# A two-layer decoder trunk on one Trainium2 core: low parts of weights made by accumulating loads, and a third pair of rows in sevens

## The chip, the cores and the metric

The program runs on one core of a Trainium2 chip. That core has a matrix engine (PE, with its weight-load half PEld), a vector engine (DVE), an activation engine (ACT), a general engine (POOL), and a queue engine (SP) that issues loads and stores. The metric is the device time in microseconds of one execution. Three executions of the kernel before took 2597.22, 2598.99 and 2599.99 us, so the median is 2598.99 us.

## The reference, cut to what matters

The reference is a trunk of two layers over 256 tokens of width 2048, all in float32. Layer 0 has a retention mixer, layer 1 a short gated convolution, and each is followed by a SwiGLU block of inner width 5632:

```
def swiglu(h, w_in, w_out):
    a, b = jnp.split(h @ w_in, 2, axis=-1)
    return (jax.nn.silu(a) * b) @ w_out
...
        x = (x + g1 * y).astype(x.dtype)
        h = (rms_norm(x, norm2_g[i]) * (1.0 + sc2) + sh2).astype(x.dtype)
        x = (x + g2 * swiglu(h, ffn_w_in[i], ffn_w_out[i])).astype(x.dtype)
    return rms_norm(x, final_g).astype(x.dtype)
```

The change is in the SwiGLU block of the last layer alone (the "last stage" below). Its input product multiplies 256 x 2048 tokens by 2048 x 11264 weights, its output product 256 x 5632 by 5632 x 2048.

## The kernel before, in words

**Three products for one.** Float32 factors are split into a high part, rounded to the type `float32r` that PE multiplies in one pass, and a low part, which is the factor minus its high part. Every product is then three: high by high, high by low and low by high (`thrice`). Activations are split once. Weights are split as they come: SP loads them from one long array, `w_all`, in blocks of 128 x 2048 (1 MB each, tile `raw`, three buffers, line L372), and `prepare` makes them ready in **pieces** of 128 x 1024. For a piece ACT copies `raw` into the tile `hi` (L402, this rounds), and DVE subtracts `hi` from `raw` into the tile `lo` (L405). `hi` and `lo` have four buffers each (`PART_BUFS`), and in the last stage a piece is prepared three pieces before PE takes it (`ahead_now`, `AHEAD + 1`). So ACT may begin piece n + 3 when PE has read the last of piece n - 1 and begins n.

**How the last stage is cut.** The weights are taken in **groups**. An input group gathers 1024 columns (512 of each half of the input weights) over all 2048 rows of weights. It goes through eight **row pairs** (two times 128 rows by 2 x 512 columns, which is one block of 1 MB). Part 0 has four input groups and two output groups, part 1 six input groups and two output groups. An output group has ten row pairs in part 0, twelve in part 1, where the very last group ends with three row pairs taken column by column, the tail.

**Common pairs and sevens.** A common row pair is two pieces, each with 12 matmuls of 128x512. A row pair in **sevens** (class `Seven`) is a product of two by two blocks (two halves of the tokens, two row blocks, two column blocks), done with seven block products where the plain way takes eight. That is 21 matmuls against 24. The seven block products need sums and differences of weight blocks, which DVE makes in `prepare`: a 128x1024 difference (L391) and two of 128x512 (L395, L397). Its pieces are four (numbers 2, 3, 4, 5), three of 1024 columns and one of 512, with 6, 6, 6 and 3 matmuls. They also need sums of the activations: for input pairs `made_in_sums` makes them once ahead of the first input group, for output pairs `turned` makes them as the pair's activations come out. Which pairs are in sevens is in the line

```
IN_SEVEN, OUT_SEVEN, TURNS_AT, BESIDE_CB, BESIDE_SUMS = (3, 5), (2, 4, 6), 2, 40, 48
```

**Between groups.** After the last seven of a group its four side banks are mixed (`mixed_sums`: one ACT copy, four DVE additions), after the last row pair DVE adds the four main banks (L1315), ACT takes silu twice (L1319), DVE multiplies twice (L1320). Two row pairs into the next group (`TURNS_AT`) PE turns the result with eight transposes (L1329), and ACT and DVE split it (L1333, L1334).

**What sets the order.** PE's instructions stand in the order of the program text. The instructions of ACT, DVE, POOL and SP are put into an order per engine by the framework's scheduler when the program is built. Each engine then works through its list strictly in that order, so an instruction that waits holds up all that stand behind it.

Of the kernel before, what the change touches and what calls it, by code (L numbers as in the profile page):

```python
# [10 lines left out]
F32 = mybir.dt.float32  # L11
# [3 lines left out]
ALU = mybir.AluOpType  # L15
# [162 lines left out]
def last_out(part):  # L178

    first, n = part * LAST_TILES[0], LAST_TILES[part]  # L180
    order = list(range(n // 2))
    if not part:
        a, b = order[-2:]
        order = order[:5] + [a, order[6], b, order[5], order[7]]
    rows = [(i, [first + 2 * i, first + 2 * i + 1]) for i in order]
    out = []
    for c in range(0, D, 2 * DV):
        cols, rest = [c, c + DV], 0
        if part and c + 2 * DV == D:
            rest = TAIL_ROWS // 2  # L190
        out.append(in_pairs(cols, rows[: len(rows) - rest], OUT_SEVEN))
# [65 lines left out]
def trunk(ctx: ExitStack, tc: tile.TileContext, x_in, c_in, pos_in, w_mod, cols_in, gain_in, tab_in, w_all, out):  # L257
# [12 lines left out]
    def tmp(tag, shape=(P, S), dtype=F32, pool=work, bufs=None):  # L270
        return pool.tile(list(shape), dtype, tag=tag, name=name(tag), bufs=bufs)
# [104 lines left out]
    def prepare(between=None):  # L376
        if prepared[0] == len(pieces):
            return
        _, piece = pieces[prepared[0]]
        prepared[0] += 1  # L380
        if piece in (0, 2):
            if not fetched:
                fetch()
            raws[:] = [fetched.pop(0)]
            while first <= units[0] < early and len(fetched) < RAW_BUFS - 1 and n_fetched[0] < w_all.shape[0]:
                fetch()
        whole = raws[0]
        b = [whole[:, i : i + DV] for i in range(0, CHUNK, DV)]
        raw = whole[:, :HALF] if piece in (0, 4) else whole[:, HALF:]
        if piece == 2:  # L390
            nc.vector.tensor_tensor(differences, whole[:, DV : 3 * DV], whole[:, : 2 * DV], op=ALU.subtract)  # L391
        elif piece == 3:
            raw = differences
        elif piece == 4:
            nc.vector.tensor_tensor(b[1], b[2], differences[:, :DV], op=ALU.subtract)  # L395
        elif piece == 5:
            nc.vector.tensor_tensor(b[3], b[3], b[1], op=ALU.subtract)  # L397
# [4 lines left out]
        nc.scalar.copy(hi, raw)  # L402
        if between:
            between()
        nc.vector.tensor_tensor(lo, raw, hi.bitcast(F32), op=ALU.subtract)  # L405
        ready.append((hi, lo, width))

    prepared, ahead_now = [0], [AHEAD]
# [714 lines left out]
    def turn(t, c):  # L1123
# [8 lines left out]
    needed(1, GT2)  # L1132
    in_cb = const.tile([P, D], F32R, tag="cb", name="in_cb")
    tokens_sums = [
        v.rearrange("p (i n) -> p i n", i=2) for v in (in_cb[:, : 6 * P], in_cb[:, 6 * P : 12 * P])
    ] + [mpool.tile([P, 2, 3 * P], F32R, tag="sums_of_tokens", name="sums_of_tokens")]

    def tokens_sums_of(a11, a21, a12, a22, third, others):

# [17 lines left out]
    def made_in_sums():  # L1157

        tmp("beside_sums", (P, BESIDE_SUMS), bufs=1)
        for i in IN_SEVEN:  # L1160
            both = tmp("u512", (P, 2, S), pool=mpool, bufs=3)
            for n in range(2):
                k = 2 * i + n
                high, low = [h[k].bitcast(F32)[:, v, :] for v in range(2)]
                nc.vector.tensor_tensor(both[:, n, :], high, low, op=ALU.add)
            tag = "low" if in_sums else "u"
            in_sums[i] = [tmp(tag, (P, 2, P), F32R, bufs=3) for _ in range(3)]
            tokens_sums_of(*parts(both), h[2 * i][:, :, P:], in_sums[i])

    def three(v):  # L1170
        return [v[:, :, n * P : (n + 1) * P] for n in range(3)]

    turns = [lambda t=t, c=c: turn(t, c) for c in range(4) for t in range(2)]

# [136 lines left out]
    def last_input(groups, pairs, seven):  # L1311

        ours, extra = gathered(groups, h, 0, in_sums)
        for (t, j), pt in ours.items():
            nc.vector.tensor_tensor(extra[t, j], pt, extra[t, j], op=ALU.add)  # L1315
        ms = []
        for t in range(2):
            m = extra[t, 0]
            nc.scalar.activation(m, m, AF.Silu)  # L1319
            nc.vector.tensor_tensor(m, m, extra[t, 1], op=ALU.mult)  # L1320
            ms.append(m)

        def turned():
            for n, (dst, of) in enumerate(zip(pairs, seven)):
                pt = bank()
                for i in range(2):
                    for t, m in enumerate(ms):
                        c = slice((2 * n + i) * P, (2 * n + i + 1) * P)
                        nc.tensor.transpose(pt[:, i, t * P : (t + 1) * P], m[:, c], ident)  # L1329
                if of is not None:  # L1330
                    both = tmp("u512", (P, 2, S), pool=mpool, bufs=3)
                    nc.scalar.copy(both, pt)
                nc.scalar.copy(dst[:, :, 0, :], pt)  # L1333
                nc.vector.tensor_tensor(dst[:, :, 1, :], pt, dst[:, :, 0, :].bitcast(F32), op=ALU.subtract)  # L1334
                if of is not None:
                    tokens_sums_of(*parts(both), dst[:, 0, :, P:], [of])

        waiting.append(turned)

    def last_output(part, c, groups, act, base):  # L1340
# [14 lines left out]
            for (t, j), v in extra.items():  # L1355
                gated(t, c + j, v, 0)

        sums = {i: three(v) for i, v in zip(OUT_SEVEN, tokens_sums)}
# [27 lines left out]
    for part in range(2):  # L1386
        n = LAST_TILES[part] // 2
        mid = mids(LAST_TILES[part]) if part else first_mid
        if not part:
            first_rows(mid[-2:])  # L1390
            made_in_sums()
            ahead_now[0] = AHEAD + 1
        for i, groups in enumerate(LAST_IN[part]):
            seven = [tokens_sums[OUT_SEVEN.index(q)] if q in OUT_SEVEN else None for q in (2 * i, 2 * i + 1)]
# [41 lines left out]
```

## Time and profile before

| what | value |
|---|---|
| median of three runs | 2598.99 us |
| profiled execution, its own time | 2600.71 us |
| profiled execution, span of the trace | 2598.8 us |
| last stage, first difference of weights (L391) to the span's end | from 1927.9 us on |
| granted PE clock in the profiled run | 0.999 |
| PE busy share of the span | 99% |
| DVE, ACT, POOL busy shares | 83%, 50%, 5% |

The profile is of one execution. Its span lies 1.9 us below that execution's own time and 0.2 us below the median of the three runs. Times in the trace are counted from the span's start. A matmul's duration in the rows overlaps with the next matmul's, since matmuls are pipelined, so PE's pace is read from the distance between starts and not from durations. The same is true, to a lesser degree, of DVE and ACT. A row of the waits says which instruction waited for which, then the sum in us, the number of times and the longest.

### The profile page before, as it was taken

To read this page: it belongs to the slowest core of one execution; us is meant where nothing else is said; L and a number is where in the kernel's file an instruction comes from. 1 tells how busy PE (TensorE), PEld (TensorE's weight loads), DVE (VectorE), ACT (ScalarE), POOL (GpSimd) and SP (SyncE) were. 2 spreads that over 40 slices of the span, in tenths; PEclk is the share of its full clock that TensorE was granted. 3 is DMA by queue.
4 is the path that set the end of the run, shared out by engine and by line. 5 is a ranking of instruction groups with operands and counts; after the bars stand their busy time and mean duration, and the time that the engine had idled before them with its cause. 6 is when DMAs were issued, how large, how long until landed. Compare 5 with 4: busy or idle time off the path is not lost.

```text
span 2598.8 us, 36365 instructions
## 1 busy us (share of the span) xinstructions
PE 2567.0 (99%) x14211; PEld 2241.0 (86%) x14211; DVE 2157.4 (83%) x2702; ACT 1289.4 (50%) x1768; POOL 125.7 (5%) x232
## 2 busy tenths in 40 slices
PE   7999999999999999999999999999999999999998
PEld 6898889888889888888888898888998888888886
DVE  7988978887698887777777889988988888888877
ACT  5544543444456454334444454444565554555554
POOL 0000000110000000100001001000000000000000
PEclk9999999999999999999999999999999999999999
DMA  9975668877676888787778868877845565554653
GB/s 399 387 290 221 255 246 300 299 261 276 244 284 247 330 325 305 298 299 302 294 284 296 299 237 313 326 290 277 305 171 204 190 217 203 184 207 182 221 200 146
DMA packets 96686, 689.55 MB, mean 265 GB/s; under 512 B 10737, under 2 KB 12161, under 8 KB 13441
## 3 DMA queue, kind: packets, MB, share of 16 engines
q1 hardware_dynamic: 96514, 687.23, 71.1%
q8 instruction: 111, 1.82, 0.3%
q14 instruction: 61, 0.50, 0.1%
HBM read 685.08 MB, written 2.11 MB: 264 GB/s over the span
## 4 chain that ended last, share of the span: by engine, by line
PE 84%; DVE 7%; DMA 5%; issue 2%; ACT 1%; ACTq 0%; POOLq 0%; POOL 0%; DVEq 0%; SPq 0%
PE bank L447 25%; PE bank L450 14%; PE bank L461 12%; PE bank L460 12%; PE bank L462 12%; DMA raw<-w_all 4%; DVE lo L405 3%; DMA raw<-w_mod 2%; PE bank L496 2%; PE bank L495 1%; PE bank L494 1%; PE bank L627 1%; PE bank L629 1%; PE bank L628 1%; DVE raw L755 1%
## 5 line engine op out<-in xcount | busy, mean ns | idle before, releaser
L402 ACT CAST hi<-raw 128x1024 fp32r<-128x1024 f32 (+1 forms) x944 | 973.1, 1039 | 1037.0 <-PE bank L462 385.6
L405 DVE TENSOR_TENSOR lo<-raw,hi 128x1024 fp32r<-128x1024 f32 (+1 forms) x944 | 1129.9, 1203 | 347.4 <-ACT hi L402 340.0
L447 PE MATMUL bank<-h,hi 128*128 128x512 f32 x2016 | 699.2, 390 | 0.0
L450 PE MATMUL bank<-h,lo 128*128 128x256 f32 x2016 | 568.4, 282 | 0.0
L447 PEld LDWEIGHTS bank<-h,hi 128*128 128x128 f32 x2016 | 378.3, 188 | 79.2
L460 PE MATMUL bank<-hi,h 128*128 128x512 f32 x1072 | 420.1, 392 | 1.8 <-DVE rm L739 1.8
L461 PE MATMUL bank<-lo,h 128*128 128x512 f32 x1072 | 418.3, 390 | 0.7 <-DVE lo L405 0.7
L462 PE MATMUL bank<-hi,h 128*128 128x512 f32 x1072 | 417.6, 390 | 0.0
L318 DVE SCALAR_TENSOR_TENSOR raw<-raw,cb 128x2048 f32<-128x2048 f32 x160 | 365.6, 2285 | 23.2 <-DMA raw<-w_mod 22.9
L450 PEld LDWEIGHTS bank<-h,lo 128*128 128x128 f32 x2016 | 381.0, 189 | 0.0
L447 PE MATMUL bank<-mid,hi 128*128 128x512 f32 x922 | 319.8, 390 | 0.0
L450 PE MATMUL bank<-mid,lo 128*128 128x256 f32 x922 | 260.1, 282 | 0.4 <-DVE lo L405 0.4
L462 PEld LDWEIGHTS bank<-hi,h 128*128 128x128 f32 x1072 | 201.4, 188 | 42.6
L460 PEld LDWEIGHTS bank<-hi,h 128*128 128x128 f32 x1072 | 201.8, 188 | 41.8 <-DVE rm L739 2.4
L461 PEld LDWEIGHTS bank<-lo,h 128*128 128x128 f32 x1072 | 201.9, 188 | 39.9 <-DVE lo L405 1.1
L447 PEld LDWEIGHTS bank<-mid,hi 128*128 128x128 f32 x922 | 173.0, 188 | 36.2
L450 PEld LDWEIGHTS bank<-mid,lo 128*128 128x128 f32 x922 | 174.3, 189 | 0.7 <-DVE lo L405 0.7
L447 PE MATMUL bank<-rm,hi 128*128 128x512 f32 x496 | 172.6, 390 | 0.0
L496 PE MATMUL bank<-h,lo 128*128 128x256 f32 x512 | 146.2, 286 | 5.2 <-DVE lo L405 5.2
L494 PE MATMUL bank<-h,hi 128*128 128x256 f32 x512 | 145.6, 284 | 3.2 <-ACT h L783 3.2
L495 PE MATMUL bank<-h,hi 128*128 128x256 f32 x512 | 145.6, 284 | 0.7 <-DVE h L784 0.7
L450 PE MATMUL bank<-rm,lo 128*128 128x256 f32 x496 | 139.9, 282 | 0.0
(248 smaller groups left out, 3092.4 us busy)
## 6 DMA issues: line engine op xcount, KB each, us to landing
raw<-w_all SPq DMA_DIRECT2D x456, 1024.0 KB, 4.9
raw<-w_mod SPq DMA_DIRECT2D x192, 1024.0 KB, 5.3
x<-x_in SPq DMA_DIRECT2D x4, 512.0 KB, 5.5
out<-xt SPq DMA_DIRECT2D x4, 512.0 KB, 3.0
decay<-tab_in SPq DMA_DIRECT2D x8, 128.0 KB, 2.7
x<-gate_row SPq DMA_DIRECT2D x2, 512.0 KB, 4.4
last_gain<-gain_in SPq DMA_DIRECT2D x1, 1024.0 KB, 4.6
cols<-cols_in SPq DMA_DIRECT2D x1, 152.0 KB, 8.5
```

The source lines that it names most:

```text
L318: nc.vector.scalar_tensor_tensor(raw, raw, 1.0, cb, op0=ALU.mult, op1=ALU.mult, accum_out=total)
L402: nc.scalar.copy(hi, raw)
L405: nc.vector.tensor_tensor(lo, raw, hi.bitcast(F32), op=ALU.subtract)
L447: nc.tensor.matmul(pt, hi, h, start=fresh and k == g.ks[0], stop=False, skip_group_check=True)
L450: nc.tensor.matmul(pt[:, 1, :], lo, h[:, 0, :], start=False, stop=last and k == g.ks[-1], skip_group_check=True)
L460: nc.tensor.matmul(o, hi, w_hi, start=first, stop=False)
L461: nc.tensor.matmul(o, hi, w_lo, start=False, stop=False)
L462: nc.tensor.matmul(o, lo, w_hi, start=False, stop=last)
L494: nc.tensor.matmul(pt, hi, h[:, 0, :], start=first, stop=False, skip_group_check=True)
L495: nc.tensor.matmul(pt, hi, h[:, 1, :], start=False, stop=False, skip_group_check=True)
L496: nc.tensor.matmul(pt, lo, h[:, 0, :], start=False, stop=last, skip_group_check=True)
L627: nc.tensor.matmul(pt, hi, high, start=k == 0, stop=False, skip_group_check=True)
```

## The change

Two things are edited together.

- **More row pairs in sevens.** Input pairs 3, 4 and 6 of each group (3 and 5 before). Output pairs 2, 4, 5 and 6 in part 0 and 2, 4, 6 and 8 in part 1 (2, 4 and 6 in both before). That is one more pair in each of the ten input and four output groups. The sums of activations that these need get tiles of their own, out of buffers that are free in this stage.
- **Low parts by accumulating loads.** For a common piece whose three predecessors are common too, from the stage's third block on (`low_by_dma`), `lo` is made without DVE, in two halves of 512 columns: ACT copies the half of `raw` into `hi` (line L410 of the changed kernel), then writes minus that high part into `lo` (L411), and POOL issues a load of the same 128x512 weights from `w_all` that adds to what stands in `lo` (L413, 256 KB each). This holds for 66 pieces: five of the ten common pieces of an input group and some of the output groups, so 132 loads and 34.6 MB that are read a second time.

```diff
-IN_SEVEN, OUT_SEVEN, TURNS_AT, BESIDE_CB, BESIDE_SUMS = (3, 5), (2, 4, 6), 2, 40, 48
+IN_SEVEN, OUT_SEVEN, TURNS_AT, BESIDE_CB, BESIDE_SUMS = (3, 4, 6), ((2, 4, 5, 6), (2, 4, 6, 8)), 2, 40, 48
...
+    last_block = min(in_seven) - IN_SEVEN[0]
     pieces = [(i, p) for i in range(w_all.shape[0]) for p in ((2, 3, 4, 5) if i in in_seven else (0, 1))]
+
+    def low_by_dma(n):
+
+        return pieces[n][0] > last_block + 1 and all(p < 2 for _, p in pieces[n - 3 : n + 1])
...
-        nc.scalar.copy(hi, raw)
-        if between:
-            between()
-        nc.vector.tensor_tensor(lo, raw, hi.bitcast(F32), op=ALU.subtract)
+        if low_by_dma(prepared[0] - 1):
+            for i in range(0, width, DV):
+                v = slice(i, i + DV)
+                nc.scalar.copy(hi[:, v], raw[:, v])
+                nc.scalar.mul(lo[:, v], hi[:, v].bitcast(F32), -1.0)
+                o = piece * HALF + i
+                nc.gpsimd.dma_start(lo[:, v], w_all[block, :, o : o + DV], accum_op=ALU.add)
+        else:
+            nc.scalar.copy(hi, raw)
+            if between:
+                between()
+            nc.vector.tensor_tensor(lo, raw, hi.bitcast(F32), op=ALU.subtract)
...
+        for tag, n in (("u", 3), ("low", 3), ("sum", 4)):
+            single_sums.extend(tmp(tag, (P, 2, P), F32R, bufs=n) for _ in range(n))
         for i in IN_SEVEN:
...
-            tag = "low" if in_sums else "u"
-            in_sums[i] = [tmp(tag, (P, 2, P), F32R, bufs=3) for _ in range(3)]
+            in_sums[i] = [single_sums.pop() for _ in range(3)]
```

Ahead of the last stage the lists of all engines are the same as before, apart from line numbers. Within it, the order moves as follows. ACT's list at the passage from one input group of part 1 to the next (the `hi` of the old group's last pieces, then those of the new group's first), before:

```order
L402 CAST hi_22488<-raw_22486 128x1024
L402 CAST hi_22502<-raw_22486 128x1024
L402 CAST hi_22520<-raw_22518 128x1024
L402 CAST hi_22536<-raw_22518 128x1024
L402 CAST hi_22554<-raw_22552 128x1024
L1319 ACTIVATE x_76<-x_76 128x512
L402 CAST hi_22582<-raw_22552 128x1024
L1319 ACTIVATE x_76<-x_76 128x512
L402 CAST hi_22600<-raw_22598 128x1024
```

and the same place in the change:

```order
L415 CAST hi_22837<-raw_22835 128x1024
L410 CAST hi_22851<-raw_22835 128x512 x2
L411 ACTIVATE lo_22852<-hi_22851 128x512 x2
L410 CAST hi_22873<-raw_22871 128x512 x2
L411 ACTIVATE lo_22874<-hi_22873 128x512 x2
L1336 ACTIVATE x_76<-x_76 128x512
L410 CAST hi_22905<-raw_22871 128x512
L1336 ACTIVATE x_76<-x_76 128x512
L411 ACTIVATE lo_22906<-hi_22905 128x512
L410 CAST hi_22905<-raw_22871 128x512
L411 ACTIVATE lo_22906<-hi_22905 128x512
L410 CAST hi_22927<-raw_22925 128x512 x2
```

Each copy of 1024 columns has become four instructions of 512. The scheduler put both halves' copies ahead of both halves' negations, except where the two silu (L1336) stand between them.

DVE's list around the sevens of an input group of part 1, before (`raw_22296` is row pair 3, `raw_22388` the common pair 4, `raw_22410` pair 5):

```order
L405 TENSOR_TENSOR lo_22358<-raw_22296,hi_22357 128x1024
L405 TENSOR_TENSOR lo_22379<-raw_22296,hi_22378 128x512
L395 TENSOR_TENSOR raw_22410<-raw_22410,x_75 128x512
L405 TENSOR_TENSOR lo_22391<-raw_22388,hi_22390 128x1024
L405 TENSOR_TENSOR lo_22401<-raw_22388,hi_22400 128x1024
L405 TENSOR_TENSOR lo_22414<-raw_22410,hi_22413 128x1024
```

and in the change (L396, L400 and L402 are the differences of weights, L418 makes `lo`, rows on `x_75` use the stored 128x1024 difference; `raw_22239` is row pair 3, `raw_22331` pair 4, `raw_22373` pair 5 and `raw_22395` pair 6):

```order
L396 TENSOR_TENSOR x_75<-raw_22331 128x1024
L525 TENSOR_TENSOR in_cb<-u_4105_22267,in_cb 128x384
L418 TENSOR_TENSOR lo_22301<-raw_22239,hi_22300 128x1024
L418 TENSOR_TENSOR lo_22322<-raw_22239,hi_22321 128x512
L400 TENSOR_TENSOR raw_22331<-raw_22331,x_75 128x512
L418 TENSOR_TENSOR lo_22335<-raw_22331,hi_22334 128x1024
L402 TENSOR_TENSOR raw_22331<-raw_22331 128x512
L418 TENSOR_TENSOR lo_22345<-x_75,hi_22344 128x1024
L418 TENSOR_TENSOR lo_22356<-raw_22331,hi_22355 128x1024
L418 TENSOR_TENSOR lo_22364<-raw_22331,hi_22363 128x512
L396 TENSOR_TENSOR x_75<-raw_22395 128x1024
L418 TENSOR_TENSOR lo_22376<-raw_22373,hi_22375 128x1024
```

The sevens of pairs 3 and 4 follow each other, and the 1024-wide difference for pair 6 stands ahead of the first `lo` of the common pair 5.

POOL's list, which before held only small instructions in this stage, toward the end of the change:

```order
L413 DMA lo_23749<-w_all 128x512 x2
L413 DMA lo_23793<-w_all 128x512 x2
L1235 TENSOR_TENSOR sums<-total 128x1 x2
L413 DMA lo_24154<-w_all 128x512 x2
L413 DMA lo_24176<-w_all 128x512 x2
L413 DMA lo_24196<-w_all 128x512 x2
L1236 TENSOR_TENSOR sums<-sums,total 128x1
```

The loads of the tail's last three pieces stand behind two additions (L1235) that wait for ACT's squares of the first output group of part 1.

More of the change, by code (lines that the diff above doesn't have):

```diff
@@ L190, in last_out @@
             rest = TAIL_ROWS // 2
-        out.append(in_pairs(cols, rows[: len(rows) - rest], OUT_SEVEN))
+        out.append(in_pairs(cols, rows[: len(rows) - rest], OUT_SEVEN[part]))
         if rest:
@@ L378, in prepare @@
             return
-        _, piece = pieces[prepared[0]]
+        block, piece = pieces[prepared[0]]
         prepared[0] += 1
@@ L1165, in made_in_sums @@
                 nc.vector.tensor_tensor(both[:, n, :], high, low, op=ALU.add)
[L1166 to L1167 removed]
+            in_sums[i] = [single_sums.pop() for _ in range(3)]
             tokens_sums_of(*parts(both), h[2 * i][:, :, P:], in_sums[i])
+        if single_sums[2:]:
+            tokens_sums.append([single_sums.pop() for _ in range(3)])
     def three(v):
[L1171 removed]
+        return [v[0][:, :, n * P : (n + 1) * P] for n in range(3)] if len(v) == 1 else v
     turns = [lambda t=t, c=c: turn(t, c) for c in range(4) for t in range(2)]
@@ L1335, in turned @@
                 if of is not None:
-                    tokens_sums_of(*parts(both), dst[:, 0, :, P:], [of])
+                    tokens_sums_of(*parts(both), dst[:, 0, :, P:], of)
         waiting.append(turned)
@@ L1356, in mixed @@
                 gated(t, c + j, v, 0)
-        sums = {i: three(v) for i, v in zip(OUT_SEVEN, tokens_sums)}
+        sums = {i: three(v) for i, v in zip(OUT_SEVEN[part], tokens_sums)}
         ours, extra = gathered(groups, act, base, sums, beside, mixed if final else None)
@@ L1393, in trunk @@
         for i, groups in enumerate(LAST_IN[part]):
-            seven = [tokens_sums[OUT_SEVEN.index(q)] if q in OUT_SEVEN else None for q in (2 * i, 2 * i + 1)]
+            due = OUT_SEVEN[part]
+            seven = [tokens_sums[due.index(q)] if q in due else None for q in (2 * i, 2 * i + 1)]
             last_input(groups, mid[2 * i : 2 * i + 2], seven)
```

5 lines of the change are left out of this document (3 added, 2 removed).

## The prediction

> **What bounds the kernel now.** I read the page first, for the engines' shares and the chain.
>
> ```profile
> span 2598.8 us, 36365 instructions
> PE 2567.0 (99%) x14211; PEld 2241.0 (86%) x14211; DVE 2157.4 (83%) x2702; ACT 1289.4 (50%) x1768; POOL 125.7 (5%) x232
> PE 84%; DVE 7%; DMA 5%; issue 2%; ACT 1%; ACTq 0%; POOLq 0%; POOL 0%; DVEq 0%; SPq 0%
> ```
>
> PE is busy almost throughout and carries 84% of the chain. Since the change touches the last stage alone, I then asked for the busy time of each engine in that stage and in one input group of it. The columns are window, its length, then busy us of PE, PEld, DVE, ACT and POOL, granted clock, share and GB/s of the DMA engines.
>
> ```profile
> 1927.90:2590.00 662.10, 660.38 (x2949) 545.86 (x2947) 551.05 (x642) 348.02 (x401) 4.59 (x7) 1.00 0.53 194
> 2243.20:2286.30 43.10, 43.10 (x195) 35.76 (x195) 34.88 (x38) 22.57 (x26) 0.00 (x0) 1.00 0.55 195
> ```
>
> PE lacks only 1.72 us in 662, DVE is at 83%, ACT at 53%, POOL at nothing. A busy PE is not proof of a PE at its pace, so I looked at who waited for whom in the stage.
>
> ```profile
> ACT hi L402 <- PE bank L462: 272.2, 234, 2.0
> DVE lo L405 <- ACT hi L402: 88.3, 109, 1.5
> DVE x L391 <- DMA raw<-w_all: 5.0, 5, 2.3
> PE bank L461 <- DVE lo L405: 1.7, 3, 0.8
> ```
>
> ACT waits for PE (a free buffer), DVE for ACT, and PE for almost nothing: three times, 1.7 us in all, for a low part. So each matmul that is left out here should come off the time, as long as the weights stay ready. The pace comes from a timeline of PE: two starts of a common piece, then the turn of a result.
>
> ```profile
> 2250.51 0.39 PE L460 MATMUL bank<-hi,h 128*128 128x512 f32 x1
> ...
> 2253.23 0.39 PE L460 MATMUL bank<-hi,h 128*128 128x512 f32 x1
> ...
> 2255.96 1.03 PE L1329 MATMUL bank<-tab,x 128*128 128x128 f32 x8
> 2256.75 0.48 PE L460 MATMUL bank<-hi,h 128*128 128x512 f32 x1
> ```
>
> Twelve matmuls take 2.72 us, 0.2267 us each, and the eight transposes 0.79.
>
> **The change part by part.** *Fewer matmuls.* Fourteen groups lose three matmuls each: 42 x 0.2267 = 9.52 us, 0.68 per group. This is the whole gain that can come directly.
>
> *DVE, ACT and DMA as sums.* Durations in the stage:
>
> ```profile
> L405 DVE TENSOR_TENSOR lo<-raw,hi 128x1024 fp32r<-128x1024 f32 x244 | 296.5, 1222 | 68.2 <-ACT hi L402 63.7
> L402 ACT CAST hi<-raw 128x1024 fp32r<-128x1024 f32 x244 | 255.9, 1055 | 226.4 <-PE bank L462 207.0 <-DVE lo L405 7.7 <-issue 6.2
> L391 DVE TENSOR_TENSOR x<-raw 128x1024 f32<-128x1024 f32 x32 | 39.0, 1219 | 5.1 <-DMA raw<-w_all 5.0
> L405 DVE TENSOR_TENSOR lo<-raw,hi 128x512 fp32r<-128x512 f32 x32 | 22.1, 690 | 18.0 <-ACT hi L402 17.7
> L397 DVE TENSOR_TENSOR raw<-raw 128x512 f32<-128x512 f32 x32 | 22.0, 687 | 0.3
> L402 ACT CAST hi<-raw 128x512 fp32r<-128x512 f32 x32 | 19.9, 622 | 48.1 <-PE bank L462 41.4 <-DVE lo L405 6.6
> L1319 ACT ACTIVATE x<-x 128x512 f32<-128x512 f32 x20 | 12.7, 633 | 3.6 <-DVE x L1315 3.6
> ```
>
> A seven costs DVE 3 x 1.222 + 0.690 + 1.219 + 2 x 0.687 = 6.95 us, a common pair 2.44, so the new seven adds 4.51. Five low parts off DVE take 6.11 away. DVE goes from 34.9 to 33.3 us per input group of 42.4, still 79%. On ACT the seven adds 3 x 1.055 + 0.622 - 2 x 1.055 = 1.68. No row negates into SBUF; the nearest is silu, also an ACTIVATE of 512 columns from SBUF, 0.633. So an accumulated piece takes 2 x 0.622 + 2 x 0.633 - 1.055 = 1.46 more, five of them 7.3. ACT goes from 22.6 to 31.5 us of 42.4, 74%. Both are covered by PE. If DVE or ACT lost that cover, the price would be what its list runs late at one place, which the next two walks look for. The sums for the third input pair are 18 small operations ahead of the first group, the two further output pairs some ten more each; they stand while three pieces are ready ahead of PE (8.2 us), and I cost them at nothing (at most 2 us, once).
>
> *The accumulated pieces, walked.* Let T = 0 be PE's start on an input group. Common pieces start at 0, 2.72, 5.44, 8.16, then the turn, 11.7 and 14.4. For pace and reaction I use these rows of ACT and DVE:
>
> ```profile
> 2250.77 1.05 ACT L402 CAST hi<-raw 128x1024 fp32r<-128x1024 f32 x1 [1.68 <-PE bank L462]
> ...
> 2276.43 0.58 ACT L1240 COPY x<-bank 128x512 f32<-128x512 f32 x1
> 2276.91 2.00 ACT L402 CAST hi<-raw 128x1024 fp32r<-128x1024 f32 x2
> ```
>
> ```profile
> 2278.30 1.22 DVE L405 TENSOR_TENSOR lo<-raw,hi 128x1024 fp32r<-128x1024 f32 x1
> 2279.44 0.68 DVE L1242 TENSOR_TENSOR x<-bank,u 128x512 f32<-128x512 f32 x1
> ...
> 2281.17 0.68 DVE L1243 TENSOR_TENSOR u<-bank,x 128x512 f32<-128x512 f32 x1
> 2281.77 0.68 DVE L1244 TENSOR_TENSOR u<-bank,u 128x512 f32<-128x512 f32 x1
> ```
>
> ACT starts 0.26 after PE's piece start (2250.51 to 2250.77) that frees the buffer. Back to back, ACT needs 0.95 per 1024 columns and 0.48 to 0.62 per 512 (I take 0.55); DVE needs 1.14 and 0.60. The group's second piece is let go at T = -5.44. ACT does copy, copy, negate, negate, so the first half's load can be issued at -5.18 + 3 x 0.55 = -3.5, the second's at -3.0. PE wants the first half's low part at its second matmul, 2.72 + 0.23 = 2.95, and the second half's 1.36 later: 6.45 us and more. The next piece has the same. The fourth is the worst on ACT: the two silu stand among its four instructions, and its first half is issued at about 2.0, wanted at 8.39, 6.4 us. The fifth and sixth gain 0.8 from the turn. ACT needs 2.2 us per such piece against PE's 2.72, so it catches up. **A load thus has 6.4 us from the negation to PE.** What does it need? No row shows a load from POOL or one that adds. The nearest:
>
> ```profile
> raw<-w_all SPq DMA_DIRECT2D x110, 1024.0 KB, 4.8
> ...
> decay<-tab_in SPq DMA_DIRECT2D x8, 128.0 KB, 2.7
> ...
> raw<-w_all SPq DMA_DIRECT2D x16, 1024.0 KB, 9.4
> ```
>
> The first is from the last stage (1950 to 2540 us), the second from the page, the third from the span's first 100 us. A line through the first two gives 0.60 us per 256 KB and 3.0 us for one such load alone, an estimate. Beside a 1 MB load it may wait for that load's whole 2.4 us: 5.4. The upper bound is 9.4 us, the landing where the DMA engines had no gap. I take 5.4, nearest to the stage's own rows, since its share of DMA is 0.55: inside the 6.4, so no stall. Per group 2.6 MB are added to a share of 0.55 at 195 GB/s; 2.6 MB cost 7.4 us of all engines, so the share rises from 23.7 us in 43.1 to 31.1 in 42.4, 73%. SP's own loads leave earlier than before, since ACT and not DVE now reads `raw` last. On POOL's queue the two small additions wait for the squares of part 1's first output group, which come early in the next group; the tail's loads behind them are issued at its end, and PE, which waits for these, loses nothing.
>
> The Trainium skill ("Collectives: The Full Stack", The bandwidth ceiling: the fold count and why AG ≠ RS ≠ AR) says that an add in the DMA engines needs two source reads and so twice the read traffic of a copy. By the rows alone the load takes 5.4 us and the sum loses nothing; by this rule it takes another 0.6, 6.0 us, which leaves 0.4 for POOL to write the load's descriptors. No run here shows either yet; what would follow is the third rival.
>
> *Two sevens in a row, walked.* Pieces of sevens last 1.36 us (the last 0.68), so three pieces ahead is only some 4 us there. Pair 3 starts at T = 17.1, pair 4 at 21.9, pair 5 at 26.64. The first piece of pair 4 may be copied when PE leaves the first of pair 3, at 18.48: ACT 18.74 to 19.8. From 19.85 DVE has, in its list's order, low part 1.14, difference 0.60, low parts 1.14, 1.14 and 0.60, the 1024 difference for pair 6 (1.14), and the low part of pair 5's first piece (1.22 to its end): 26.83. PE wants that at 26.64 + 0.23 = 26.87. So it just fits. The group of part 0 that is turned with two pairs to sum (its list has about 0.6 more there) misses by some 0.5. The load that the difference for pair 6 needs leaves when DVE has done pair 3's last low part, 18.7; 4.8 later is 23.5, before the 24.5 at which DVE comes to it. I charge 0.05 to 0.1 per input group and 0.5 for the odd one, together 1.0 us.
>
> *The sum.* 9.5 - 1.0 = 8.5 us. The profiled span would go from 2598.8 to 2590.3, its execution from 2600.7 to 2592.2, and the median of the runs from 2599.0 to **2590.5 us**. Its own range is 2588 (the present 1.7 us of waits go too) to 2593.8.
>
> **Rivals.** *Late low parts.* The walk leaves 6.4 us for a load, and thirteen passages from group to group have at least three accumulated pieces each. If a load takes L, PE stands L - 6.4 at each passage, once, because the stall itself puts the later pieces' limits back. The gain is used up at L = 6.4 + 8.5 / 13 = 7.05. Midway to the saturated landing, 7.9, it costs 13 x 1.5 = 19.5 us: 2610. For it: issue on POOL is unseen, and ten such loads and three of 1 MB share the DMA engines within some 15 us. Against it: the stage's loads land in 4.8, half the saturated figure.
>
> *The three-piece lead between sevens.* The second walk fits by 0.04 us. If the load for pair 6 lands at 6 us rather than 4.8, or each hand-over from ACT to DVE costs a tenth more, the low part of pair 5 comes 0.5 to 0.9 late in each of ten input groups, 5 to 9 us: about 2597.5. For it: PE's few waits now are for just such low parts. Against it: a stall gives its length back to the next pieces.
>
> *Two reads per add.* If an adding load reads twice, it takes 5.4 + 0.6 = 6.0 us, and where POOL takes 1 us to issue it, 7.0 in all: 13 x 0.6 = 7.8 of the gain returned, 2598.3. For it: the add must read what stands in `lo`. Against it: the wait for a 1 MB load beside it was already added in full. The Trainium skill states it ("Collectives: The Full Stack", the section above).
>
> That the change doesn't take out matmuls can be excluded: PE's list is 42 shorter.
>
> **How the numbers follow.** The forecast 0.50; late low parts 0.22; the lead between sevens 0.18; two reads 0.10. About 0.2% (5.2 us) is what a measurement here can tell from no change. Faster: 0.50, and 0.02 each from the second and third rival, 0.54. Same: 0.13 of the second, 0.07 of the third, 0.01 of the first, 0.21. Slower: 0.21 of the first, 0.03 and 0.01 of the others, 0.25. The range goes from 2588 (0.05 below it) to 2610, beyond which lies half of the first rival, 0.11: 0.16 outside.
>
> **What would show it.** Right: 42 matmuls fewer, PE idle in the stage under 3 us, input groups 42.4 us from turn to turn, accumulating loads on POOL's queue that land in 5 to 6 us, DVE near 79% and ACT near 74% in a group. Late loads would show as waits of PE's second matmul of a piece (the one that reads `lo`) for a DMA; the lead between sevens as waits of the same line for DVE at pair 5; two reads as a DMA share near 0.9 in a group instead of 0.73. The prediction is wrong if PE waits for the loads more than 0.6 us per passage.

## The result, and the profile after

The change makes the kernel slower: 2695.05 us in the median of four runs (2694.84 to 2696.93) against 2598.1 of the kernel before beside it (2596.66 to 2599.99), a ratio of 1.0373, interval 1.036 to 1.0386. The forecast of 2590.5 us and its range up to 2610 both missed. The profiled execution took 2694.84 us, its span 2693.1.

The page of the changed kernel: its span and the engines' shares, the queue that POOL feeds, the chain of work by engine and by line, and the landing of the new loads. The last row holds POOL's instruction, which starts such a load.

```profile
span 2693.1 us, 36948 instructions
PE 2600.3 (97%) x14169; PEld 2245.0 (83%) x14169; DVE 2148.1 (80%) x2732; ACT 1387.2 (52%) x2008; POOL 241.5 (9%) x364
q0 software_dynamic: 19008, 34.61, 7.3%
PE 80%; DMA 10%; DVE 4%; ACT 3%; issue 2%; POOL 0%; ACTq 0%; POOLq 0%; DVEq 0%; SPq 0%
lo<-w_all POOLq DMA_DIRECT2D x132, 256.0 KB, 10.8
L413 POOL DMA_DIRECT2D lo<-w_all x132 | 117.0, 1026 | 657.1 <-ACT lo L411 608.4
```

PE has 42 matmuls fewer, as meant. But an accumulating load lands 10.8 us after its issue, where the prediction took 5.4 and had 6.4 to give. The DMA's part of the chain rose from 5% to 10%.

The waits of the last stage in the changed kernel (who waited for whom, us in all, times, longest). `L474` is the matmul that reads `lo`; PEld is its weight load, and a weight load's wait and its matmul's wait overlap in part, so the two are not added.

```profile
PEld bank L474 <- DMA lo<-w_all: 91.2, 60, 4.1
PE bank L474 <- DMA lo<-w_all: 64.8, 54, 3.7
DVE x L396 <- DMA raw<-w_all: 36.2, 20, 10.9
PEld bank L474 <- DVE lo L418: 4.2, 11, 0.7
PE bank L474 <- DVE lo L418: 0.4, 2, 0.2
```

The matmuls wait 54 times for an accumulating load, for DVE almost never. The next view is the busy time of the engines in three stretches: the stage, one group's 24 us from its first accumulating load to the landing of its last, and the 19 us of sevens behind it (columns as in the prediction, the last three being granted clock, DMA share and GB/s).

```profile
1927.90:2683.00 755.10, 689.65 (x2899) 546.68 (x2898) 539.42 (x667) 444.56 (x637) 120.10 (x139) 0.97 0.74 215
...
2287.00:2311.00 24.00, 20.98 (x86) 16.00 (x85) 12.50 (x17) 13.73 (x24) 8.83 (x10) 0.93 1.06 276
2311.00:2330.00 19.00, 19.00 (x84) 15.41 (x83) 16.11 (x17) 10.76 (x13) 0.00 (x0) 1.00 0.44 166
```

Over the stage the DMA engines' share is 0.74, almost the 0.73 that the prediction worked out for a group. Where the loads are, it is 1.06 (packets overlap a little, so a full share can read above 1), and in the sevens 0.44. The mean hid a stretch in which the DMA engines are full.

What one wait does, on PE's timeline in that stretch:

```profile
2292.30 0.39 PE L475 MATMUL bank<-hi,h 128*128 128x512 f32 x1
2292.53 0.39 PE L473 MATMUL bank<-hi,h 128*128 128x512 f32 x1
2294.85 0.50 PE L474 MATMUL bank<-lo,h 128*128 128x512 f32 x1 [1.93 <-DMA lo<-w_all]
2295.18 0.40 PE L475 MATMUL bank<-hi,h 128*128 128x512 f32 x1
...
2296.23 0.63 PE L475 MATMUL bank<-hi,h 128*128 128x512 f32 x1
2296.66 0.63 PE L473 MATMUL bank<-hi,h 128*128 128x512 f32 x1
2297.08 0.63 PE L474 MATMUL bank<-lo,h 128*128 128x512 f32 x1
```

A little after the wait the starts are 0.43 us apart, not 0.23. The granted clock in this stretch (0.57 in the mean of these 4 us; the clock records have one half for 3.41 of them) goes with that:

```profile
2295.00:2299.00 4.00, 4.00 (x11) 3.17 (x12) 1.35 (x2) 0.00 (x0) 1.48 (x2) 0.57 1.09 326
```

From the starts of all matmuls and the clock records of the stage, its 94.2 us more (661.5 to 755.7, first start to last) divide up as follows: 9.5 less for the matmuls left out; 78.9 more in distances between starts that are over 60 ns above the usual 227, at full clock; 23.8 more while the granted clock is one half, in ten stretches of 51.2 us together. That is 93.2; the remaining microsecond lies in small differences.

### The profile page after: what moved, and what is told of

It is laid out like the page before. It is cut to its first block, busy times and chain, and to the rows that moved or that the text cites. A ratio compares the mean times of both kernels' runs of the same rounds, so it can differ in the third digit from the quotient of the medians.

```text
span 2693.1 us, 36948 instructions
## 1 busy us (share of the span) xinstructions
PE 2600.3 (97%) x14169; PEld 2245.0 (83%) x14169; DVE 2148.1 (80%) x2732; ACT 1387.2 (52%) x2008; POOL 241.5 (9%) x364
## 4 chain that ended last, share of the span: by engine, by line
PE 80%; DMA 10%; DVE 4%; ACT 3%; issue 2%; POOL 0%; ACTq 0%; POOLq 0%; DVEq 0%; SPq 0%
PE bank L460 27%; PE bank L463 15%; PE bank L474 9%; PE bank L475 9%; PE bank L473 9%; DMA lo<-w_all 8%; DMA raw<-w_all 2%; PE bank L509 2%; PE bank L507 2%; PE bank L508 2%; DVE lo L418 1%; PE bank L640 1%; PE bank L642 1%; PE bank L641 1%; DVE raw L768 1%
## 5 line engine op out<-in xcount | busy, mean ns | idle before, releaser
L415 ACT CAST hi<-raw 128x1024 fp32r<-128x1024 f32 x892 | 912.0, 1029 | 958.1 <-PE bank L460 310.5
L418 DVE TENSOR_TENSOR lo<-raw,hi 128x1024 fp32r<-128x1024 f32 x892 | 1057.0, 1193 | 395.1 <-ACT hi L415 390.0
L474 PE MATMUL bank<-lo,h 128*128 128x512 f32 x1032 | 415.1, 402 | 41.4 <-DMA lo<-w_all 40.9
L473 PE MATMUL bank<-hi,h 128*128 128x512 f32 x1032 | 410.8, 398 | 1.7 <-DVE rm L752 1.7
L475 PE MATMUL bank<-hi,h 128*128 128x512 f32 x1032 | 408.8, 396 | 0.0
L474 PEld LDWEIGHTS bank<-lo,h 128*128 128x128 f32 x1032 | 197.8, 192 | 99.0 <-DMA lo<-w_all 57.2
L473 PEld LDWEIGHTS bank<-hi,h 128*128 128x128 f32 x1032 | 197.8, 192 | 42.0 <-DVE rm L752 2.3
L475 PEld LDWEIGHTS bank<-hi,h 128*128 128x128 f32 x1032 | 197.7, 192 | 40.5
L413 POOL DMA_DIRECT2D lo<-w_all x132 | 117.0, 1026 | 657.1 <-ACT lo L411 608.4
## 6 DMA issues: line engine op xcount, KB each, us to landing
lo<-w_all POOLq DMA_DIRECT2D x132, 256.0 KB, 10.8
```

The source lines that it names most:

```text
L413: nc.gpsimd.dma_start(lo[:, v], w_all[block, :, o : o + DV], accum_op=ALU.add)
L473: nc.tensor.matmul(o, hi, w_hi, start=first, stop=False)
L474: nc.tensor.matmul(o, hi, w_lo, start=False, stop=False)
L475: nc.tensor.matmul(o, lo, w_hi, start=False, stop=last)
```

## The experiments

All edits below are made in the changed kernel. The theories: the loads come late because of the DMA engines (what an adding load costs there, what else they carry, in which order); because of POOL's own path (a fixed delay before a load starts); or the loss is the third seven's and its DVE work. A fourth question was whether fewer accumulated pieces would fit. Times of the kernel before beside each group of runs: 2598.2 us (the first four), 2598.49 (the next three), 2597.84 (the last four).

| run | what it is | us | ratio to before, interval |
|---|---|---|---|
| e1 | third seven, no accumulating load | 2591.5 | 0.9974, 0.9964 to 0.9984 |
| e2 | two sevens, 66 accumulated pieces | 2681.36 | 1.0319, 1.0302 to 1.0337 |
| e3 | the change, loads that don't add | 2632.32 | 1.0125, 1.0107 to 1.0142 |
| e4 | 24 accumulated pieces (6th and 8th of a run) | 2612.35 | 1.0057, 1.0043 to 1.0071 |
| e5 | 24 accumulated pieces (5th and 7th) | 2643.81 | 1.0171, 1.0157 to 1.0185 |
| e6 | 10 accumulated pieces (7th) | 2634.64 | 1.014, 1.0126 to 1.0155 |
| e7 | the change, loads of 512 KB | 2707.59 | 1.042, 1.0401 to 1.044 |
| e8 | as e6, SP's loads in 2 KB packets | 2613.38 | 1.006, 1.0045 to 1.0075 |
| e9 | the change, SP's loads in 2 KB packets | 2713.01 | 1.0445, 1.0429 to 1.0461 |
| e10 | as e1, SP's loads in 2 KB packets | 2603.42 | 1.0021, 1.0012 to 1.0031 |
| e11 | as e6, SP's loads in 4 KB packets | 2607.43 | 1.0035, 1.0023 to 1.0047 |

**Each half of the change alone.** First the third seven, with every low part on DVE:

```diff
 def low_by_dma(n):
 
-    return pieces[n][0] > last_block + 1 and all(p < 2 for _, p in pieces[n - 3 : n + 1])
+    return False
```

> The changed kernel with the third pair in sevens kept and every low part made by DVE again. Theory A (the accumulating loads are late because the DMA engines can't carry ten of them in a row beside the 1 MB loads: each holds all 16 engines for about 1.46 us, 128 packets of 178 ns): all waits for loads go, DVE has 39.4 of 42.4 us per input group, time 2592 to 2605 us. Rival B (a load from POOL takes some 10 us whatever else runs): the same here. Rival C (the third seven is what costs, by DVE or by the lead between sevens): stays above 2650 us.

It took 2591.5 us, 6.7 less than before. Its waits for DVE and its stage:

```profile
PEld bank L474 <- DVE lo L418: 6.0, 12, 1.7
PE bank L474 <- DVE lo L418: 1.8, 3, 1.3
...
1927.90:2580.00 652.10, 650.34 (x2898) 535.65 (x2896) 605.76 (x730) 370.28 (x436) 15.32 (x6) 1.00 0.54 195
```

The stage is 10.0 us shorter than before (651.5 against 661.5), the predicted 9.5 and half a microsecond. DVE is busy 605.76 of 652.10 us, 93%, and PE waits for it 1.8 us, as before. The profiled span is 8.5 us shorter (2590.3 against 2598.8), because what follows the start of the stage's last matmul takes 10.7 us instead of 9.3; the medians differ by 6.7 us, interval 4.2 to 9.4. So the sevens gain about what was forecast for them, and they need no relief on DVE. This is the fastest kernel of the study.

Then the loads with the pairs in sevens as before:

```diff
-IN_SEVEN, OUT_SEVEN, TURNS_AT, BESIDE_CB, BESIDE_SUMS = (3, 4, 6), ((2, 4, 5, 6), (2, 4, 6, 8)), 2, 40, 48
+IN_SEVEN, OUT_SEVEN, TURNS_AT, BESIDE_CB, BESIDE_SUMS = (3, 5), ((2, 4, 6), (2, 4, 6)), 2, 40, 48
...
-    return pieces[n][0] > last_block + 1 and all(p < 2 for _, p in pieces[n - 3 : n + 1])
+    run = 0
+    while run <= n and pieces[n - run][1] < 2:
+        run += 1
+    return pieces[n][0] > last_block + 1 and 6 <= run <= 10
```

> Sevens as in the kernel before (two per input group, three per output group), and 66 common pieces with accumulating loads, five per input group (there the same pieces as in the change). Theory A and rival B: landings again near 11 us, time 2670 to 2700 us, 42 matmuls (9.5 us) of it for the sevens that are gone. Rival C: within 10 us of the kernel before.

It took 2681.36 us, 83 more than before, and PE's wait for the loads is much like the change's:

```profile
PEld bank L477 <- DMA lo<-w_all: 88.6, 60, 3.0
PE bank L477 <- DMA lo<-w_all: 63.2, 56, 2.6
```

The loss belongs to the accumulating loads; the third seven isn't needed for it. Beside the third seven the loads cost some 20 us more (103.6 above e1, where here it is 83 above the kernel before). Most of that is half clock: 23.8 us lost by it in the change's profiled execution, 8.0 in e2's. Why the clock fell more often there isn't shown.

**The addition.** The loads stay, but without the adding; this kernel leaves the subtraction out, so `lo` holds the whole weight.

```diff
-                nc.gpsimd.dma_start(lo[:, v], w_all[block, :, o : o + DV], accum_op=ALU.add)
+                nc.gpsimd.dma_start(lo[:, v], w_all[block, :, o : o + DV])
```

> The changed kernel with the same 132 loads from POOL that overwrite instead of adding; it leaves out the addition, so the low parts are whole weights and the output is not the reference's, while bytes, instructions and queue stay. Theory A: a packet of 2 KB takes some 80 to 90 ns instead of 178, a load 0.7 us of the engines, landing 5 to 6.5 us, time 2592 to 2615 us. Rival B: landing stays at 10 to 11 us and the time above 2670 us.

It took 2632.32 us: 62.7 of the 103.6 us between e1 and the change are gone, 40.8 remain. Its page and its waits:

```profile
q0 software_dynamic: 19008, 34.61, 4.4%
lo<-w_all POOLq DMA_DIRECT2D x132, 256.0 KB, 7.3
L413 POOL DMA_DIRECT2D lo<-w_all x132 | 70.9, 541 | 649.3 <-ACT lo L411 599.8 <-DVE low L525 48.3 <-DVE x L396 1.2
...
PE bank L474 <- DMA lo<-w_all: 31.2, 19, 2.5
```

The same packets and bytes take 4.4% of the engines instead of 7.3%. In the trace's packet records a 2 KB packet that adds takes 178 ns in the median, one that doesn't 99. POOL's instruction takes 541 ns instead of 1026 in the mean. Even so a plain load of POOL's lands at 7.3 us, still too late for a limit of 6.4: the expected landing of 5 to 6.5 and time of 2592 to 2615 were missed. So the add is more than half of the loss, and not all of it.

**Fewer accumulated pieces.** In these three only the last line of `low_by_dma` differs; `run` counts the common pieces since the last seven, as in e2.

```diff
+    return pieces[n][0] > last_block + 1 and run in (6, 8)
```

> The changed kernel with accumulating loads for the sixth and the eighth common piece in a run alone: two of ten pieces of an input group, 24 pieces in all, at least 5 us apart. Theory A: two halves take 2.9 us of the engines between 1 MB loads of 2.6 us, landing 4.5 to 6.5 us, few waits for loads, DVE near 37 of 42.4 us per input group, time 2590 to 2600 us. Rival B: landing stays near 10 us, 22 passages with 3 to 4 us of wait each, time above 2650 us. Rival C: above 2650 us for its sevens.

2612.35 us, 20.9 more than e1 and above the expected 2600; landing 7.7, expected 4.5 to 6.5. PE waits for the loads 14.9 us, and no clock is lost.

```diff
+    return pieces[n][0] > last_block + 1 and run in (5, 7)
```

> As the run with two of ten, but for the fifth and the seventh common piece in a run (first pieces of a block) in place of the sixth and the eighth (second pieces): again 24 pieces, 48 loads, 5 us apart. The copies of a second piece free the weights' buffer, so that a 1 MB load starts together with the accumulating ones; those of a first piece don't. Theory A in its form after the first runs (a load waits for whatever is queued on the DMA engines, its own part is 1.43 us, some 1.8 us from issue to the first packet): packets end 4.5 to 6 us after the issue instead of 6 to 9, landing 5 to 6.5 us, waits of PE for loads under 5 us in all (14.9 there), time 2590 to 2600 us. If lateness doesn't come from the 1 MB loads beside them: landing stays at 7.7 us and the time at 2612 us.

2643.81 us, a miss: as many pieces, one place earlier, cost 52 us instead of 21. The place alone more than doubles the loss.

```diff
+    return pieces[n][0] > last_block + 1 and run == 7
```

> The changed kernel with an accumulating load for the seventh common piece of a run alone: ten pieces, 20 loads, one piece per input group. Theory A: two halves alone, landing 4.5 to 6 us, no waits for loads, time as with sevens alone (2589 to 2593 us), since the 1.22 us that DVE saves per group are not on the path. If every load from POOL is late: ten waits of 1 us and more, 2600 us or above.

2634.64 us, another miss: ten pieces, one to a run of common pieces, cost 43 us, 4.3 each, although no other accumulated piece is near. The mean DMA share around it is low:

```profile
2303.00:2350.00 47.00, 43.86 (x189) 35.42 (x188) 38.20 (x47) 26.24 (x33) 1.77 (x2) 0.96 0.54 183
```

and yet both halves of the piece are late. PE's timeline, then ACT's, then POOL's:

```profile
2315.47 0.48 PE L476 MATMUL bank<-hi,h 128*128 128x512 f32 x1
2316.88 0.50 PE L477 MATMUL bank<-lo,h 128*128 128x512 f32 x1 [0.93 <-DMA lo<-w_all]
...
2318.13 0.39 PE L476 MATMUL bank<-hi,h 128*128 128x512 f32 x1
2320.73 0.79 PE L477 MATMUL bank<-lo,h 128*128 128x512 f32 x1 [2.21 <-DMA lo<-w_all]
```

```profile
2308.32 1.15 ACT L414 ACTIVATE lo<-hi 128x512 fp32r<-128x512 f32 x2
```

```profile
2309.24 1.77 POOL L416 DMA_DIRECT2D lo<-w_all  x2 [44.53 <-ACT lo L414]
```

From the first negation's end (about 2308.9) to PE's wish for the first half (2315.7) it is 6.8 us: the walk's 6.4 was right. From the packet records, in us after the load's instruction starts on POOL:

```
                                    first packet   last packet
e6 (8 KB packets on SP's queue), first half   1.58   6.97
                                 second half  6.25  10.24
e11 (4 KB), first half                        1.59   5.36
            second half                       5.09   7.79
e8 (2 KB),  first half                        1.58   4.92
            second half                       4.74   6.99
```

(one input group of each, each half counted from its own issue; the two are issued 0.55 us apart.) In e6 the first half's first packet is there 1.58 us after the issue, so POOL's path is short when the DMA engines are idle. But a load that lasts 1.45 us when alone lasts 5.4 and 4.0 here. SP issues 1 MB loads 0.6 and 2.8 us after POOL's first one, so both queues are live at once. A packet of SP's is 8 KB and takes 309 ns. If each engine takes one packet from either queue in turn, the eight packets that a half load has on each engine take 8 x (0.178 + 0.309) = 3.9 us, which is what the second half took (6.25 to 10.24). A count in the records agrees: between the first and the last packet of a half, each engine starts 8.0 (first half) and 8.2 (second) of SP's packets. In the first half the first packets of SP's last longer, 0.9 us in the mean, which goes with the 5.4. The next runs test that.

**The packets of SP's loads.** The same bytes in smaller packets, for the last stage only (2 KB here, with `HALF` in place of `DV` 4 KB):

```diff
-        nc.sync.dma_start(raw, w_all[n_fetched[0]])
+        cut = DV if n_fetched[0] > last_block + 1 else CHUNK
+        for i in range(0, CHUNK, cut):
+            nc.sync.dma_start(raw[:, i : i + cut], w_all[n_fetched[0], :, i : i + cut])
```

> The kernel with one accumulated piece per run of common pieces (the seventh; 2634.6 us), with SP's 1 MB loads of the last stage cut into four loads of 128x512, so that their packets are 2 KB instead of 8 KB. Nothing else is changed, and the bytes are the same. Theory A (the engines take packets of the two queues in turn: in that run's trace a half load lasted 4.0 to 5.4 us beside 1 MB loads and 1.45 us alone; 8 turns of 0.178 + 0.309 us are 3.9): 8 turns of 0.178 + 0.099 us are 2.2, so the first half's last packet comes 4 to 5 us after its issue instead of 6.95, the second's after 6.5 to 7.5 instead of 10.3; waits of PE for lo from a DMA under 5 us in the stage instead of 27 to 34, no window of half clock, 2592 to 2600 us. Theory B (it is the bytes that lie ahead, whatever their packets, or POOL's path itself): landing stays near 7.8 us median and the time within 2628 to 2640.

> As the run with one accumulated piece and cut loads, but cut in two (128x1024, 4 KB packets). Theory A: between the two, a turn of 0.178 + about 0.16 us (between the measured 0.099 for 2 KB and 0.309 for 8 KB), 8 of them 2.7 us: first half's last packet after 5 to 5.7 us, second's after 8 to 8.7; 2603 to 2622 us. Theory B: 2628 to 2640 as with whole loads.

> The control: the third seven alone (2591.5 us, no accumulating load), with the same cut of SP's loads. Theory A and B: no accumulating load, nothing waits, 2590 to 2594 us. If the cut itself costs or gains more than that, it is taken off the other two runs.

The packet times came out near what the turn-taking gave: in the groups of the table the halves end after 4.9 and 7.0 us with 2 KB (4 to 5, and 6.5 to 7.5, expected), after 5.4 and 7.8 with 4 KB (5 to 5.7, and 8 to 8.7; the other groups have 7.8 to 9.0 for the second half). The turns are less strict there: each engine starts 8 to 16 of SP's packets during a half. PE's waits for the loads in e11 and, behind the dots, in e8:

```profile
PEld bank L479 <- DMA lo<-w_all: 15.2, 11, 2.5
PE bank L479 <- DMA lo<-w_all: 10.5, 10, 2.0
```

```profile
PEld bank L479 <- DVE lo L423: 17.3, 24, 1.8
PEld bank L479 <- DMA lo<-w_all: 9.0, 11, 2.3
PE bank L479 <- DVE lo L423: 7.9, 10, 1.3
PE bank L479 <- DMA lo<-w_all: 4.2, 5, 1.9
```

27.2 us of PE's waits in e6 became 10.5 and 4.2, by nothing but how another queue's loads are cut. The total of e8 missed its 2592 to 2600, because the control e10 missed too: cutting SP's loads into 2 KB costs 11.9 us by itself (2603.42 against 2591.5 in e1). There the DMA share of the stage rises from 0.54 to 0.62, ACT and DVE wait for SP's loads (in e1 DVE waits 0.4 us for them), and PE then for DVE:

```profile
ACT hi L417 <- DMA raw<-w_all: 23.8, 9, 3.0
DVE x L398 <- DMA raw<-w_all: 16.5, 11, 3.0
PEld bank L476 <- DVE lo L420: 16.4, 22, 1.7
PE bank L476 <- DVE lo L420: 7.7, 12, 1.3
...
1927.90:2580.00 652.10, 644.94 (x2861) 527.89 (x2860) 596.21 (x718) 368.93 (x435) 1.91 (x2) 1.00 0.62 196
```

So what one accumulated piece per run costs is 43.1 us beside 8 KB packets (e6 less e1) and 10.0 beside 2 KB (e8 less e10). For 4 KB there was no control; its 15.9 above e1 is an upper figure if the cut into 4 KB costs nothing or more.

**Volume.** The same cut with all 66 pieces, and the change with a piece's two loads made one of 512 KB:

> The change itself (2695 us) with SP's 1 MB loads of the last stage cut into four loads of 128x512 (2 KB packets). Theory A (packets in turn): the accumulating queue gets 0.178 of 0.277 of each engine's time instead of 0.178 of 0.487 while SP loads too, so the first loads of a group come 2 to 4 us earlier; but ten loads of 1.46 us and three of 1 MB still fill the DMA engines for some 24 us, so the later ones stay late: landing 7 to 9 us median instead of 10.8, 2630 to 2665 us. Theory B (bytes ahead or POOL's path): landing 10 to 11 us, 2685 to 2705.

```diff
-            for i in range(0, width, DV):
-                v = slice(i, i + DV)
+            for i in range(0, width, HALF):
+                v = slice(i, i + HALF)
...
-                nc.gpsimd.dma_start(lo[:, v], w_all[block, :, o : o + DV], accum_op=ALU.add)
+                nc.gpsimd.dma_start(lo[:, v], w_all[block, :, o : o + HALF], accum_op=ALU.add)
```

> The changed kernel with its 66 accumulating loads of 128x1024 in one instead of two halves of 128x512. Theory A: the same bytes twice read, so a packet of 4 KB takes some 300 to 360 ns, the DMA engines carry as much as before, and a piece has no early half: landing 11 to 14 us, time 2690 to 2740 us. If packets had a fixed cost that the halves double: packets of 4 KB near 200 ns, landing near 7 us, time below 2650 us.

Smaller packets on SP's queue don't help the whole change: 2713.01 us, 18 more, of which the cut's own price explains some 12, landing 11.2. The expected 2630 to 2665 was wrong. Larger packets of the adding loads don't help either: 2707.59 us in two runs, landing 10.8; a 4 KB packet that adds takes 328 ns, so the price goes nearly by the byte, and a piece comes only when all of it is there. With ten loads to a group it is, by the sum that follows, the engines' whole work that binds, not the order of their packets.

The work in the group shown, from 2286.93 (first issue) to 2311.07 (last packet, 24.1 us): ten loads of eight packets of 0.178 us on each engine, 14.2 us; and 488 packets of 8 KB, 30.5 on each engine, 9.4 us. Together 23.6 of 24.1. By the prediction's own walk PE wants the last half 4 x 2.72 + 0.79 + 1.36 + 6.45 = 19.5 us after the first issue. So a group is some 4.6 us short, 5.3 with the 0.7 us that pass from the last packet to PE's start. There are 66 / 5 = 13.2 such groups' worth of pieces: 70 us, against the 78.9 counted in the starts. This is an estimate, but it is of the right size. The work itself could have been estimated ahead, save the 0.178: the prediction had the ten loads, and rows of 1 MB loads and their GB/s.

A lead of four pieces was not tried.

## Why the prediction was wrong

**The gain was right.** 42 x 0.2267 = 9.5 us are there: e1's stage is 10.0 us shorter, its median 6.7. The 1.0 us that was charged for two sevens in a row doesn't show as a wait, and the rival of the three-piece lead is out: PE waits for DVE 0.4 us in the change, 1.8 in e1. What the prediction did not ask is whether the accumulating loads buy anything. It worked out 4.51 us more per group for a seven on DVE and 6.11 less for the loads. Without the loads DVE is at 93% of the stage, and PE covers that.

**The walk's 6.4 us from the negation to PE held.** e6 shows 6.8 for the one piece timed above.

**The step that failed is the landing of an accumulating load, "I take 5.4".** It measured 10.8, above even the upper bound of 9.4. Three things were wrong in it.

- The 5.4 was made as 0.60 us of its own and one 1 MB load's 2.4 us ahead of it, on 2.4 of start. The load's own time on the engines is 1.42 us, because it adds: 0.178 us a packet against 0.099. So the rival of two reads was right that the add costs time on the engines, 1.8 times a plain load and not twice. The Trainium skill ("Collectives: The Full Stack", The bandwidth ceiling: the fold count and why AG ≠ RS ≠ AR) puts the price of an add in a collective down to a second source read; 1.8 is near its factor of two, but no record here counts reads. And the rival charged only 0.6 us for it, as if a load had no others behind it.
- A 1 MB load was taken to be in front of it, at 2.4 us, or not. In e4 and e5 that is what the records show: where SP's load is issued 0.3 to 0.9 us before, the first packet of the adding load comes 3.2 to 4.7 us after its issue instead of 1.58. But where SP's load is issued just after, as in e6, the loads run side by side and packets are taken in turn, 2 KB against 8 KB, so the accumulating queue gets 0.178 of every 0.487 us. The waits of PE follow: 27.2, 10.5 and 4.2 us for 8, 4 and 2 KB (e6, e11, e8). The Trainium skill ("DMA: Bandwidth & Descriptors", Queues, rings and completion order) says that each engine goes round the queues packet by packet, where a packet is typically 9 to 17 descriptors; it would have spoken against the step. The going round is borne out by e6's count of 8.0 and 8.2, but there the turns are of one 2 KB or 8 KB record of the trace each.
- "73%" was a mean over a group. The loads are issued within 15 us, and in those 24 us the share is 1.06. The row of the saturated landing, 9.4, was named as the upper bound and thought far. It was the nearer one, and queueing behind one's own kind goes beyond it: in the group shown, the second half of the second piece has its first packet 8.6 us after its issue.

**"Once per passage" was wrong.** The rival of late low parts was the right case, with the chance of 0.22. Its rule, 13 x (L - 6.4), gives 13 x 4.4 = 57 us for L = 10.8, 2648 with the forecast. But it has PE wait once a passage, because a stall gives later pieces their time back. It does so only if the later loads are not late themselves; here the queue falls behind with each, and PE waits 54 times, not 13.

**A term was missing: the clock.** A stall was charged at its length. Here 23.8 of the 94.2 us are matmuls at half clock after a stall. With the 23.8 and the 78.9 of waits, less the 9.5, the stage comes out within 1 us of what was measured.

Why e4's loads fare better than e5's and e6's can be read from the packet records, though no run moved SP's loads by themselves. One input group of each (the pieces issued at 2296.62, 2302.06, 2302.80, 2308.24 and 2309.24), times in us from the issue of the piece's first half; the last column is how many of SP's packets each engine starts during a half:

```
                SP's 1 MB loads  first half      second half     SP's packets,
                issued at        first, last     first, last     first / second
e4, 6th piece   -0.8, 4.6        3.41,  5.97     5.79,  7.65     0.2 / 2.1
e4, 8th piece   -0.8             4.24,  6.68     6.50,  8.75     1.5 / 0.0
e5, 5th piece   -0.9, 5.1        3.68,  6.30     6.13,  8.06     0.1 / 2.2
e5, 7th piece   -0.3, 3.1        4.32,  6.98     6.75, 11.77     2.0 / 8.1
e6, 7th piece    0.6, 2.8        1.58,  6.97     6.79, 10.79     8.0 / 8.2
```

An adding load that comes behind a 1 MB load waits for it once and then has the engines nearly to itself. One that has a 1 MB load issued some 3 us behind its own issue shares with it packet by packet, and its second half ends 3 to 4 us later. The seventh piece is in that place, the fifth, sixth and eighth are not. e5's expectation had it the other way round: it took the second pieces of a block to be those that start a 1 MB load beside them. Why the two queues take turns in one case and not in the other stays open.

## What to carry to other kernels

Cost a burst of transfers by the work on the DMA engines within the burst: packets times their durations, of every queue that is live then, against the time until the last is wanted; a mean share over a longer stretch can hide the burst. Before work is moved off an engine, ask whether that engine was in anyone's way: here DVE at 93% cost PE nothing, and the relief cost 104 us. And a wait of PE can have two prices, its length and the slow matmuls after it.

## What the runs showed that was not expected

- **The clock falls after short gaps.** Each of the ten half-clock stretches in the changed kernel's stage begins 2.6 to 3.9 us after the start of the last matmul ahead of a gap; the shortest of these gaps is the one shown above, 2.32 us from start to start and 1.93 us of idle time. Each lasts 3.41 us, or two or three times that. Sixteen distances between starts were 2.0 us or more, so not every gap does it; e4 had one such and lost no clock. The kernel before, e1 and e10 have no such distance in the stage, and no stretch of half clock there. The Trainium skill ("TensorE: Matmul & The Clock Gate", Part 1) tells of a free-running window of about 3.4 us with half clock after an idle one; the length of the stretches agrees, but eight of the ten gaps were shorter than the window (the other two had 3.6 and 3.7 us of idle time).
- **A queue's packet size sets its share beside another queue when both start together.** 8 KB packets beside 2 KB ones made a load of 1.45 us last 4.0 to 5.4.
- **Fewer loads can cost more.** 48 accumulating loads cost 21 us (e4), 20 of them 43 (e6): a load with big ones issued just behind it is worse off than two with a big one ahead.
- **Cutting a 1 MB load into four costs time** even where no adding load competes: 11.9 us in e10, with the DMA share at 0.62 in place of 0.54, and ACT and DVE waiting 23.8 and 16.5 us for these loads.
